# One addition per pair for the halo columns of an up-projection's convolution, with their products made once per block

## The chip, the cores and the metric

The kernel runs on one core of a Trainium2 chip. The metric is the device time of one execution in microseconds, the median of three runs. TensorE (PE) multiplies matrices, VectorE (DVE), ScalarE (ACT) and GpSimd (POOL) work element by element, SyncE (SP) issues the DMAs.

## The reference, cut to what matters

One layer of a bidirectional encoder over 2048 positions with width 1024: a mixer of windowed attention and a state space scan, then a feed-forward part with a convolution over positions. The change touches the feed-forward part:

```python
def dwconv(u, w, b):
    """Centred depthwise conv over positions. u (B,S,C), w (K,C), b (C,)."""
...
  h = rmsnorm(x, norm2_g[l])
  u = dwconv(h @ w_up[l].astype(h.dtype), ffn_conv_w[l], ffn_conv_b[l])
  gate, val = jnp.split(u, 2, axis=-1)
  x = x + (jax.nn.silu(gate) * val) @ w_down[l].astype(h.dtype)
```

The convolution has three taps (FFN_CONV = 3), D_FF is 2816, all in float32. An output position needs its own column of h @ w_up, the one before and the one after.

## The kernel before

Positions lie along the free axis, in four blocks of TB = 512 (j = 0 to 3). For each block the feed-forward part goes through 22 pairs of 128 channels (NPAIR), a gate half and a value half each, in six groups. The four parts of a pair's way are:

- **Weights.** `next_w` (L145) keeps two weight tiles ahead. `w_split` (L130) makes two tiles of each raw tile: ACT casts the high part (`whi`, L141), then POOL, for a few early tiles DVE, subtracts it from the raw one for the low part (`wlo`, L142). Each tag has two buffers, so a new `whi` starts when PE has finished with the one two before.
- **Product.** `up_mm` (L1046) makes two banks of 512 columns for a pair, each from 8 x 3 matmuls: high by high (L106), high weight by low input (L107), low weight by high input (L108).
- **Convolution.** `up_unit` (L1056) has the three taps and the bias. The sum is kept one position behind, so column t of the tile `fa` is position t - 1 of the block: an activation on ACT takes the middle tap and the bias (L1067), and two scalar_tensor_tensor of 128x510 and 128x511 on DVE the others (`tap`, L1065). The first two columns of `fa` also need the last two columns of the block before, kept in `hal` for each pair and half (copied by L1079). For j > 0 two more taps, of 128x2 and 128x1, add them in (L1071 and L1072, both recorded as L1065). The last block makes one more column (L1074).
- **Gate.** ACT makes the tanh of the gate half (L1087), DVE two products (L1088, L1089), and `tail` splits the result into a high part `f` (ACT, L1092) and a low one (DVE, L1093). `flush` puts a pair's tail behind the next pair's taps.

Between these, `pace` steps the attention and the scan of the next block, whose instructions share all engines. Down-projections (`dn_b`, `dn`), the output projection of the next block (`wo_b`, with its split input `m_hi`, `m_lo`, L989 and L990) and its norm follow each other at the end of a block. The tile framework orders each engine's queue with a timeline of its own, from the program's order and the estimated times; on the chip each engine takes its queue in order, and semaphores stand between engines.

Of the kernel before, what the change touches and what calls it, by code (L numbers as in the profile page):

```python
# [10 lines left out]
F32 = mybir.dt.float32  # L11
F32R = mybir.dt.float32r
AF = mybir.ActivationFunctionType
ALU = mybir.AluOpType
# [3 lines left out]
P = 128  # L18
# [9 lines left out]
NPAIR = DFF // P  # L28
# [29 lines left out]
def block_kernel(ctx: ExitStack, tc: tile.TileContext, a: dict, out: bass.AP):  # L58
    nc = tc.nc

    cpool = ctx.enter_context(tc.tile_pool(name="cpool", bufs=1))
# [9 lines left out]
    def const(name, shape):  # L71
        t = cpool.tile(shape, F32, tag=name, name=name)
        nc.sync.dma_start(t, a[name])
        return t
# [11 lines left out]
    ptot = cpool.tile([P, 6, H], F32, tag="ptot", name="ptot")  # L86
    sv, pv, lv = (cpool.tile([P, 8, 2], F32, tag=n, name=n) for n in ("sv", "pv", "lv"))
    hal = cpool.tile([P, NPAIR, 2, 2], F32, tag="hal", name="hal")

    def dram(name, shape):  # L90
        return dpool.tile(shape, F32, tag=name, name=name)
# [19 lines left out]
    V, G, A, T = nc.vector, nc.gpsimd, nc.scalar, nc.tensor  # L111
# [176 lines left out]
    def flush():  # L288
        for f in pend:
            f()  # L290
        pend.clear()
# [6 lines left out]
    fcw = const("fcw", [P, NPAIR, 2, 4])  # L298
# [757 lines left out]
    def up_unit(j, pr, fs, idx, ps):  # L1056
        last = j == NB - 1
        acc = tpool.tile([P, 2 * FW], F32, tag="t1024", name=f"fa{j}_{pr}", bufs=5)
        acc = acc.rearrange("p (i n) -> p i n", i=2)
        for i in range(2):  # L1060
            w = lambda q: fcw[:, pr, i, q : q + 1]
            ai, u = acc[:, i], ps[i]

            def tap(o, q, src):
                V.scalar_tensor_tensor(o, src, w(q), o, ALU.mult, ALU.add)  # L1065

            A.activation(ai[:, 0:TB], u, AF.Identity, bias=w(3), scale=w(2))  # L1067
            tap(ai[:, 2:TB], 0, u[:, 0 : TB - 2])
            tap(ai[:, 1:TB], 1, u[:, 0 : TB - 1])
            if j > 0:  # L1070
                tap(ai[:, 0:2], 0, hal[:, pr, i, 0:2])  # L1071
                tap(ai[:, 0:1], 1, hal[:, pr, i, 1:2])  # L1072
            if last:
                V.tensor_scalar(  # L1074
                    ai[:, TB : TB + 1], u[:, TB - 1 : TB], w(1), w(3), ALU.mult, ALU.add
                )
                tap(ai[:, TB : TB + 1], 0, u[:, TB - 2 : TB - 1])
            else:
                V.tensor_copy(hal[:, pr, i], u[:, TB - 2 : TB])  # L1079
        n = TB  # L1080
        if last:
            n = FW
            V.memset(acc[:, :, TB + 1 : FW], 0.0)
        flush()

        th = t512(f"fth{j}_{pr}")
        A.activation(th[:, :n], acc[:, 0, :n], AF.Tanh)  # L1087
        V.scalar_tensor_tensor(th[:, :n], th[:, :n], 1.0, acc[:, 0, :n], ALU.add, ALU.mult)  # L1088
        V.tensor_tensor(th[:, :n], th[:, :n], acc[:, 1, :n], ALU.mult)  # L1089

        def tail():
            A.copy(fs[:, idx, 0, :n], th[:, :n])  # L1092
            V.tensor_tensor(fs[:, idx, 1, :n], th[:, :n], fs[:, idx, 0, :n].bitcast(F32), ALU.subtract)  # L1093

        pend.append(tail)

    def down_unit(j, g, cp, fs, w):
        k0, nk = GROUPS[g]
# [258 lines left out]
    def start_side(j):  # L1357
        side.clear()
        due[:] = [0.0, 0.0]
        if j == NB:  # L1360
            return None
        m = new_mixed(j)
        side.extend([(chunks(attn, j, m), RATE[0]), (chunks(ssd, j, m), RATE[1])])
        return m
# [19 lines left out]
    for j in range(NB):  # L1384
        more = j + 1 < NB
        if j > 0:
            mx = start_side(j + 1)
        fss = []
        for g, (k0, nk) in enumerate(GROUPS):
            fs = big.tile([P, SLOT], F32R, tag="big", name=f"f{j}_{g}").rearrange(  # L1390
# [2 lines left out]
            i = 0  # L1393
            if j == 0 and g == 0 and UP2:
# [9 lines left out]
                i = 2  # L1404
# [118 lines left out]
```

## Time and profile before

| what | value |
|---|---|
| runs before | 2463.56, 2461.11, 2459.13 us; median 2461.11 |
| profiled execution, its own time | 2459.2 us |
| its span in the trace | 2457.1 us |
| DVE taps on `hal` | 264, 101 us |
| mean granted clock of TensorE | 0.987 |

The time of the profiled execution is 2.1 us above its span. A row of the trace names the line, the engine, the operation, the tiles written and read with buffer numbers left out, and the shape; a wait is put down to the instruction whose semaphore came last. In a timeline a number in brackets is the idle time of that engine just before the instruction, with what ended it.

### The profile page before, as it was taken

The numbers are of one execution on the slowest core, as the hardware profiler recorded it, in microseconds if no ns is written. First come the engines' busy times: TensorE is split into PE (matmuls) and PEld (weight loads), VectorE is DVE, ScalarE is ACT, GpSimd is POOL, SyncE is SP. The second block draws the span as 40 slices with busy tenths as digits, with TensorE's granted clock in tenths as the row PEclk, the third lists the DMA queues.
The fourth block names the chain that finished last, engine by engine and source line by source line (L and its number), as shares of the span: only waits on it lengthen the run. The fifth ranks groups of instructions, "written<-read, shape, count | busy, mean of one in ns | idle before, by whom it ended". The sixth has DMA issues, their size and how long they took to land.

```text
span 2457.1 us, 31337 instructions
## 1 busy us (share of the span) xinstructions
PE 2347.2 (96%) x11440; PEld 1955.7 (80%) x11440; DVE 1687.5 (69%) x3056; ACT 1075.5 (44%) x1818; POOL 1086.0 (44%) x585
## 2 busy tenths in 40 slices
PE   8999999897999999999999999999999999999997
PEld 6878797776788878778787877787888877788887
DVE  5757777777886684569877675698776556844445
ACT  5444656345454443435443443354444333433334
POOL 1114314463644544455444454555444436544444
PEclk9999999998999999999999999999999999999999
DMA  6567445883444333334434333343342232333332
GB/s 229 166 194 221 134 148 181 253 274 115 130 129 126 117 125 101 124 93 152 123 117 128 122 112 116 92 153 118 114 129 90 86 121 85 121 103 95 95 92 80
DMA packets 172461, 325.82 MB, mean 133 GB/s; under 512 B 12690, under 2 KB 83730, under 8 KB 172308
## 3 DMA queue, kind: packets, MB, share of 16 engines
q1 hardware_dynamic: 172308, 323.83, 41.8%
q8 instruction: 90, 1.47, 0.2%
q14 instruction: 63, 0.52, 0.1%
HBM read 277.77 MB, written 44.71 MB: 131 GB/s over the span
## 4 chain that ended last, share of the span: by engine, by line
PE 45%; DVE 14%; POOL 2%; ACT 2%; issue 2%; DMA 1%; DVEq 0%; POOLq 0%; ACTq 0%
PE up_b L108 8%; PE up_b L107 8%; PE up_b L106 8%; DVE fa L1065 4%; PE dn_b L106 3%; PE dn_b L107 3%; PE dn_b L108 3%; PE dn L107 2%; PE dn L106 2%; PE dn L108 2%; PE wo_b L108 2%; PE wo_b L106 2%; PE wo_b L107 2%; POOL wlo L142 1%; DVE ab L893 1%
## 5 line engine op out<-in xcount | busy, mean ns | idle before, releaser
L142 POOL TENSOR_TENSOR wlo<-wraw,whi 128x1024 fp32r<-128x1024 f32 (+1 forms) x306 | 738.2, 2413 | 895.4 <-ACT whi L141 837.6
L108 PE MATMUL up_b<-h_hi,wlo 128*128 128x512 f32 x1392 | 551.7, 396 | 14.7 <-POOL wlo L142 14.7
L106 PE MATMUL up_b<-h_hi,whi 128*128 128x512 f32 x1392 | 551.3, 397 | 3.4 <-ACT whi L141 2.3
L107 PE MATMUL up_b<-h_lo,whi 128*128 128x512 f32 x1392 | 549.2, 395 | 1.9 <-DVE h_lo L208 1.9
L141 ACT CAST whi<-wraw 128x1024 fp32r<-128x1024 f32 (+1 forms) x330 | 338.9, 1027 | 467.6 <-PE up_b L107 120.9
L1065 DVE SCALAR_TENSOR_TENSOR fa<-up_b,fcw,fa 128x511 f32<-128x511 f32 (+2 forms) x396 | 271.7, 687 | 211.2 <-ACT fa L1067 206.7
L108 PEld LDWEIGHTS up_b<-h_hi,wlo 128*128 128x128 f32 x1392 | 262.4, 189 | 77.7 <-POOL wlo L142 21.1
L106 PEld LDWEIGHTS up_b<-h_hi,whi 128*128 128x128 f32 x1392 | 261.9, 188 | 62.7 <-ACT whi L141 4.9
L107 PEld LDWEIGHTS up_b<-h_lo,whi 128*128 128x128 f32 x1392 | 262.1, 188 | 60.0 <-DVE h_lo L208 3.4
L106 PE MATMUL dn_b<-f,whi 128*128 128x512 f32 x528 | 211.4, 400 | 0.4 <-DVE x L1108 0.2
L107 PE MATMUL dn_b<-f,whi 128*128 128x512 f32 x528 | 208.7, 395 | 0.0
L108 PE MATMUL dn_b<-f,wlo 128*128 128x512 f32 x528 | 204.2, 397 | 0.0
L1092 ACT CAST f<-fth 128x512 fp32r<-128x512 f32 (+1 forms) x88 | 54.6, 620 | 216.5 <-DVE fth L1089 175.5
L1087 ACT ACTIVATE fth<-fa 128x512 f32<-128x512 f32 (+1 forms) x88 | 55.6, 632 | 212.6 <-DVE fa L1065 167.6
L1108 DVE TENSOR_TENSOR x<-x,dn_b 128x512 f32<-128x512 f32 x144 | 97.6, 681 | 59.9 <-PE dn_b L108 59.6
L1067 ACT ACTIVATE fa<-up_b,fcw 128x512 f32<-128x512 f32 x176 | 135.9, 773 | 0.2
L106 PEld LDWEIGHTS dn_b<-f,whi 128*128 128x128 f32 x528 | 99.8, 189 | 22.9 <-DVE x L1108 1.1
L108 PEld LDWEIGHTS dn_b<-f,wlo 128*128 128x128 f32 x528 | 99.3, 188 | 22.5 <-POOL wlo L142 0.2
L107 PEld LDWEIGHTS dn_b<-f,whi 128*128 128x128 f32 x528 | 99.2, 188 | 21.0
L893 DVE SCALAR_TENSOR_TENSOR ab<-ab,ldt,mask 128x128 f32<-128x128 f32 x256 | 95.3, 442 | 21.8 <-DMA ab<-acs_d 21.8
L1065 DVE SCALAR_TENSOR_TENSOR fa<-hal,fcw,fa 128x2 f32<-128x2 f32 (+1 forms) x264 | 101.0, 383 | 4.6
L1093 DVE TENSOR_TENSOR f<-fth,f 128x512 fp32r<-128x512 f32 (+1 forms) x88 | 78.9, 897 | 30.9 <-ACT f L1092 30.1
(333 smaller groups left out, 4880.4 us busy)
## 6 DMA issues: line engine op xcount, KB each, us to landing
wraw<-in_w_up SPq DMA_DIRECT2D x176, 512.0 KB
wraw<-in_w_dn SPq DMA_DIRECT2D x64, 512.0 KB
wraw<-in_w_out SPq DMA_DIRECT2D x36, 512.0 KB
ab<-acs_d SPq DMA_DIRECT2D x32, 512.0 KB
wraw<-in_w_ch SPq DMA_DIRECT2D x28, 512.0 KB
wraw<-in_w_dn SPq DMA_DIRECT2D x32, 384.0 KB
ak<-ks_d SPq DMA_DIRECT2D x14, 768.0 KB
xt<-in_x SPq DMA_DIRECT2D x16, 512.0 KB
```

The source lines that it names most:

```text
L106: nc.tensor.matmul(ps, whi, xhi, start=first, stop=False)
L107: nc.tensor.matmul(ps, whi, xlo, start=False, stop=False)
L108: nc.tensor.matmul(ps, wlo, xhi, start=False, stop=last)
L141: A.copy(hi[:, :m], raw[:, :m])
L142: (V if i < WV or i in WVS else G).tensor_tensor(lo[:, :m], raw[:, :m], hi[:, :m].bitcast(F32), ALU.subtract)
L893: (G if i < SUBP[0 if first else 1] else V).scalar_tensor_tensor(ab[:, i, d], ab[:, i, d], ldt[:, d, c, h : h + 1], mask3[:, 2 * d * P : ( ...
L1065: V.scalar_tensor_tensor(o, src, w(q), o, ALU.mult, ALU.add)
L1067: A.activation(ai[:, 0:TB], u, AF.Identity, bias=w(3), scale=w(2))
L1087: A.activation(th[:, :n], acc[:, 0, :n], AF.Tanh)
L1092: A.copy(fs[:, idx, 0, :n], th[:, :n])
L1093: V.tensor_tensor(fs[:, idx, 1, :n], th[:, :n], fs[:, idx, 0, :n].bitcast(F32), ALU.subtract)
L1108: V.tensor_tensor(xv, xv, ps[i], ALU.add)
```

## The change

A second tile `cor` holds, for each pair and half, what the block before adds to the first two columns: `hal` column 0 by tap weight 0 plus `hal` column 1 by tap weight 1 for column 0, and `hal` column 1 by tap weight 0 for column 1. `halo_cor` makes it for all 22 pairs and both halves with three instructions on DVE ahead of each block j > 0, the second of which writes over the first column of `hal`. In `up_unit` one addition of 128x2x2 for both halves takes the place of the four taps, behind the loop over the halves.

```diff
+    cor = cpool.tile([P, NPAIR, 2, 2], F32, tag="cor", name="cor")
...
             tap(ai[:, 1:TB], 1, u[:, 0 : TB - 1])
-            if j > 0:
-                tap(ai[:, 0:2], 0, hal[:, pr, i, 0:2])
-                tap(ai[:, 0:1], 1, hal[:, pr, i, 1:2])
             if last:
...
             else:
                 V.tensor_copy(hal[:, pr, i], u[:, TB - 2 : TB])
+        if j > 0:
+            V.tensor_tensor(acc[:, :, 0:2], acc[:, :, 0:2], cor[:, pr], ALU.add)
         n = TB
...
+    def halo_cor():
+        m = NPAIR * 2
+        hv, cv = (t.rearrange("p a i q -> p (a i) q") for t in (hal, cor))
+        wv = fcw.rearrange("p a i q -> p (a i) q")
+        V.tensor_tensor(cv, hv, wv[:, :, 0:1].broadcast_to([P, m, 2]), ALU.mult)
+        V.tensor_tensor(hv[:, :, 0:1], hv[:, :, 1:2], wv[:, :, 1:2], ALU.mult)
+        V.tensor_tensor(cv[:, :, 0:1], cv[:, :, 0:1], hv[:, :, 0:1], ALU.add)
...
             mx = start_side(j + 1)
+            halo_cor()
```

The engines' orders move with it. DVE, pair 5 of block 1 (`fa_5` is its convolution, `fth_5` its tanh and products, `up_5_b` its two banks), before:

```order
L1065 SCALAR_TENSOR_TENSOR fa_5_9930<-hal,fcw,fa_5_9930 128x2
L1065 SCALAR_TENSOR_TENSOR fa_5_9930<-hal,fcw,fa_5_9930 128x1
L1079 COPY hal<-up_5_b_9880 128x2
L1088 SCALAR_TENSOR_TENSOR fth_5_9945<-fth_5_9945,fa_5_9930 128x512
L1065 SCALAR_TENSOR_TENSOR fa_5_9930<-up_5_b_9881,fcw,fa_5_9930 128x510
L798 TENSOR_TENSOR mixed_9190<-po_1_9724,ao_1_9951 64x2x128 x2
L1065 SCALAR_TENSOR_TENSOR fa_5_9930<-up_5_b_9881,fcw,fa_5_9930 128x511
L1065 SCALAR_TENSOR_TENSOR fa_5_9930<-hal,fcw,fa_5_9930 128x2
L808 TENSOR_REDUCE ass_9957<-asq_9955 128x128
L1065 SCALAR_TENSOR_TENSOR fa_5_9930<-hal,fcw,fa_5_9930 128x1
L1079 COPY hal<-up_5_b_9881 128x2
L1089 TENSOR_TENSOR fth_5_9945<-fth_5_9945,fa_5_9930 128x512
```

The taps on `hal` follow each half's long taps. The same queue now:

```order
L1066 SCALAR_TENSOR_TENSOR fa_5_9919<-up_5_b_9869,fcw,fa_5_9919 128x511
L1077 COPY hal<-up_5_b_9869 128x2
L924 TENSOR_TENSOR ab_1_10054<-ab_1_10054 128x4x128
L1066 SCALAR_TENSOR_TENSOR fa_5_9919<-up_5_b_9870,fcw,fa_5_9919 128x510
L1066 SCALAR_TENSOR_TENSOR fa_5_9919<-up_5_b_9870,fcw,fa_5_9919 128x511
L1077 COPY hal<-up_5_b_9870 128x2
L1079 TENSOR_TENSOR fa_5_9919<-fa_5_9919,cor 128x2x2
L1088 SCALAR_TENSOR_TENSOR fth_5_9931<-fth_5_9931,fa_5_9919 128x512
L940 TENSOR_TENSOR yt_1_9851<-yo_1_9852,ea_9325 128x512
L1089 TENSOR_TENSOR fth_5_9931<-fth_5_9931,fa_5_9919 128x512
```

The first product (L1088), which stood between the halves, now stands behind both. ACT for the same pair, before:

```order
L1067 ACTIVATE fa_5_9930<-up_5_b_9880,fcw 128x512
L1092 CAST f_1_9746<-fth_4_9824 128x512
L877 ACTIVATE ea_10871<-nacs 128x16
L1087 ACTIVATE fth_5_9945<-fa_5_9930 128x512
L141 CAST whi<-wraw 128x1024
L1067 ACTIVATE fa_5_9930<-up_5_b_9881,fcw 128x512
L795 COPY ao_1_9951<-po_1_9724 64x512
L806 ACTIVATE asq_9955<-mixed_9190 128x512
L141 CAST whi<-wraw 128x1024
L1092 CAST f_1_9746<-fth_5_9945 128x512
```

The tanh stands ahead of a `whi` and the second activation. The same queue now:

```order
L1068 ACTIVATE fa_5_9919<-up_5_b_9869,fcw 128x512
L899 ACTIVATE ab_0_10052<-ab_0_10052 128x1024
L899 ACTIVATE ab_1_10054<-ab_1_10054 128x1024
L142 CAST whi<-wraw 128x1024
L1068 ACTIVATE fa_5_9919<-up_5_b_9870,fcw 128x512
L1087 ACTIVATE fth_5_9931<-fa_5_9919 128x512
L878 ACTIVATE ea_10839<-nacs 128x16
L1092 CAST f_1_9738<-fth_5_9931 128x512
L142 CAST whi<-wraw 128x1024
```

The tanh stood between the two activations of its pair; now it stands behind both, and `f` of the same pair stands ahead of the next `whi`. DVE at the end of block 1, with the changed kernel's three new instructions (L1101 to L1103); before, the last two taps on `hal` of pair 21 stood behind the last `m_lo` there:

```order
L991 SCALAR_TENSOR_TENSOR m_lo<-mixed_9191,gv,m_hi 128x512 x2
L1116 TENSOR_TENSOR x_1_8691<-x_1_8691,dn_4_1_b_12572 128x512
L991 SCALAR_TENSOR_TENSOR m_lo<-mixed_9191,gv,m_hi 128x512
L1079 TENSOR_TENSOR fa_21_12510<-fa_21_12510,cor 128x2x2
L1116 TENSOR_TENSOR x_1_8691<-x_1_8691,dn_4_1_b_12573 128x512
L1101 TENSOR_TENSOR cor<-hal,fcw 128x88
L1088 SCALAR_TENSOR_TENSOR fth_21_12522<-fth_21_12522,fa_21_12510 128x512
L1102 TENSOR_TENSOR hal<-hal,fcw 128x44
L1089 TENSOR_TENSOR fth_21_12522<-fth_21_12522,fa_21_12510 128x512
L1103 TENSOR_TENSOR cor<-cor,hal 128x44
L1093 TENSOR_TENSOR f_5_12283<-fth_21_12522,f_5_12283 128x512
L1030 TENSOR_TENSOR x_2_12602<-x_2_12602,wo_0_b_12618 128x512
```

They stand between the instructions of the block's last pair, ahead of the first addition of the output projection.

## Rows read from the trace of the kernel before

**Rows 1.** Page, part 1: busy time, share, instructions of each engine.

```profile
PE 2347.2 (96%) x11440; PEld 1955.7 (80%) x11440; DVE 1687.5 (69%) x3056; ACT 1075.5 (44%) x1818; POOL 1086.0 (44%) x585
```

**Rows 2.** Up-projections of blocks 1-3: PE, PEld, DVE, ACT, POOL busy; clock; DMA share, GB/s.

```profile
1100.00:1490.00 390.00, 380.48 (x1755) 310.98 (x1753) 300.59 (x580) 174.74 (x308) 186.72 (x98) 1.00 0.39 124
1593.00:1983.00 390.00, 384.48 (x1779) 314.53 (x1778) 287.86 (x570) 177.96 (x312) 185.03 (x95) 1.00 0.37 115
2066.00:2406.00 340.00, 337.57 (x1831) 291.37 (x1832) 187.46 (x421) 122.80 (x157) 157.10 (x70) 0.99 0.33 100
```

**Rows 3.** Waits of PE in those stretches: us in total, times, longest.

```profile
PE up_b L108 <- POOL wlo L142: 4.0, 4, 1.7
PE up_b L106 <- ACT whi L141: 1.6, 2, 1.0
...
PE up_b L108 <- POOL wlo L142: 2.2, 3, 1.0
PE up_b L106 <- ACT whi L141: 0.7, 1, 0.7
...
PE up_b L108 <- POOL wlo L142: 4.3, 3, 2.8
```

**Rows 4.** Timeline, block 1, 1167 to 1182: start us, us, what, [idle before].

```profile
1167.70 3.60 DVE L1065 SCALAR_TENSOR_TENSOR fa<-hal,fcw,fa 128x2 f32<-128x2 f32 x2
...
1168.90 2.39 POOL L142 TENSOR_TENSOR wlo<-wraw,whi 128x1024 fp32r<-128x1024 f32 x1
...
1177.01 0.63 ACT L1087 ACTIVATE fth<-fa 128x512 f32<-128x512 f32 x1 [4.05 <-DVE fa L1065]
...
1177.54 1.03 ACT L141 CAST whi<-wraw 128x1024 fp32r<-128x1024 f32 x1
...
1178.62 0.50 PE L106 MATMUL up_b<-h_hi,whi 128*128 128x512 f32 x1 [0.64 <-ACT whi L141]
...
1181.08 0.50 PE L108 MATMUL up_b<-h_hi,wlo 128*128 128x512 f32 x1 [1.03 <-POOL wlo L142]
```

**Rows 5.** DVE's groups by form: busy us, mean ns of one | idle before.

```profile
L1065 DVE SCALAR_TENSOR_TENSOR fa<-hal,fcw,fa 128x1 f32<-128x1 f32 x132 | 54.3, 412 | 2.5
...
L1089 DVE TENSOR_TENSOR fth<-fth,fa 128x512 f32<-128x512 f32 x66 | 52.8, 800 | 0.0
...
L1065 DVE SCALAR_TENSOR_TENSOR fa<-hal,fcw,fa 128x2 f32<-128x2 f32 x132 | 46.8, 354 | 2.1
...
L1079 DVE COPY hal<-up_b 128x2 f32<-128x2 f32 x132 | 20.5, 155 | 2.7
```

**Rows 6.** Instructions on the tile hal: durations in ns, min/median/max.

```profile
L1065 DVE SCALAR_TENSOR_TENSOR fa<-hal,fcw,fa x264: 201/219/2339, 1100.1 to 2410.2; 128x2 f32<-128x2 f32 x131, 128x1 f32<-128x1 f32 x1
```

**Rows 7.** Two small additions on DVE, lines 769 and 760: ns min/median/max.

```profile
L769 DVE TENSOR_TENSOR rsm<-rsm,es x32: 149/161/2371, 285.6 to 1898.6; 128x4 f32<-128x4 f32 x32
...
L760 DVE TENSOR_TENSOR es<-vecs,mxs x32: 148/1425/2364, 282.9 to 1895.0; 128x4 f32<-128x4 f32 x32
```

**Rows 8.** Timeline, block 1, 1182 to 1185.

```profile
1182.53 2.41 POOL L142 TENSOR_TENSOR wlo<-wraw,whi 128x1024 fp32r<-128x1024 f32 x1 [1.51 <-ACT whi L141]
1182.76 2.20 DVE L1065 SCALAR_TENSOR_TENSOR fa<-hal,fcw,fa 128x1 f32<-128x1 f32 x1
```

**Rows 9.** Waits of PE from 1080 on: the one ahead of the output projection.

```profile
PE wo_b L106 <- DVE x L1108: 10.4, 2, 5.2
```

**Rows 10.** Timeline of a quiet pair at the end of block 1.

```profile
1489.78 0.83 ACT L141 CAST whi<-wraw 128x768 fp32r<-128x768 f32 x1 [0.29 <-PE up_b L107]
...
1491.33 1.53 DVE L1065 SCALAR_TENSOR_TENSOR fa<-up_b,fcw,fa 128x510 f32<-128x510 f32 x2 [1.11 <-ACT fa L1067]
...
1493.46 0.63 ACT L1087 ACTIVATE fth<-fa 128x512 f32<-128x512 f32 x1 [2.17 <-DVE fa L1065]
...
1495.33 0.83 ACT L141 CAST whi<-wraw 128x768 fp32r<-128x768 f32 x1 [1.23 <-PE up_b L107]
```

**Rows 11.** Page, part 5: the cast f on ACT.

```profile
L1092 ACT CAST f<-fth 128x512 fp32r<-128x512 f32 (+1 forms) x88 | 54.6, 620 | 216.5 <-DVE fth L1089 175.5
```

## The prediction

> **What bounds the kernel now.** I read the page's busy shares first. TensorE (PE) is busy 2347.2 of 2457.1 us, VectorE (DVE) 69% [rows 1]. So the question is not how much DVE work the change removes, but how much of PE's idle time is caused by it. The change acts only in the blocks j = 1, 2, 3, after about 1075 us; ahead of that the kernel is the same. The table of busy time by stretch, cut to the three up-projection stretches, comes next [rows 2]: PE is idle for 390 - 380.48 = 9.5 us, 390 - 384.48 = 5.5 us and 340 - 337.57 = 2.4 us, 17.4 us in all, at a granted clock of 1.00, 1.00 and 0.99 (2.4 GHz). DVE is busy 77%, 74% and 55% there. That 17.4 us is nearly all there is to win in these stretches.
>
> Then the list of PE's waits in the same stretches [rows 3]. Its largest entries are the split weights: PE waits for wlo from POOL 4.0, 2.2 and 4.3 us, and for whi from ACT 1.6 and 0.7 us, 12.8 us. In the third stretch 2.8 us of the 4.3 are one wait at the very start of the block, before any tap of that block runs. So 10.0 us in 12 waits are left, 0.8 us each. The remaining idle time of the first two stretches is attention and scan steps (9.5 - 4.0 - 1.6 = 3.9 us and 5.5 - 2.2 - 0.7 = 2.6 us).
>
> How do weights come late because of taps? The timeline shows it [rows 4]. Two taps on hal, together some 0.45 us when nothing is in the way, take 3.60 us from 1167.70 and end at 1171.30, as POOL's wlo does (1168.90 + 2.39 = 1171.29). DVE falls behind, the tanh of the next pair waits on ACT 4.05 us for a tap, the whi cast queued behind that tanh starts at 1177.54, and PE stands 0.64 us for whi and then 1.03 us for the wlo made from it. This is the path from a tap to PE: tap, tanh in ACT's queue, whi, wlo, PE.
>
> **The change part by part.** *Removed:* 264 taps on hal, four in each of the 22 pairs of three blocks: 132 of 128x2 at 354 ns and 132 of 128x1 at 412 ns [rows 5], 46.8 + 54.3 = 101.1 us of DVE. The median tap is 219 ns, the longest 2339 ns [rows 6], so 264 x 0.219 = 58 us is the work itself and 43 us is standing still as in [rows 4].
>
> *Added, 66 additions of 128x2x2.* The trace has no such instruction. The nearest are two additions of 128x4 in SBUF [rows 7], with medians of 161 and 1425 ns: 66 of them are 11 us at the one and 94 us at the other. I take the mean tap, 101.1 / 264 = 0.383 us, because the addition stands where the taps stood and, like them, reads two SBUF tiles and writes one while POOL works: 25 us.
>
> *Added, three instructions ahead of each block, nine in all* (128x88 and two of 128x44). Bounds: 0.16 us each by the faster of the two additions [rows 7] (1.4 us), 2.3 us each by the longest tap (21 us); I take 0.4 us, 4 us in all. In the order they stand behind the last m_lo of the block before, among that block's last instructions, where DVE next waits for the output projection; that wait covers them. Without that cover they would cost those 4 us, three times 1.2 us.
>
> DVE's sum: -101 + 25 + 4 = -72 us, between -89 and +14. The Trainium skill, Perfetto Trace Analysis, section Optimizing Scalar/DVE Operations, gives about 60 ns of overhead for a DVE instruction on SBUF; by that figure 189 fewer instructions would be an estimated 11 us, and the sum would be a sixth of mine; here the rows show 219 ns and more for one.
>
> *What of it reaches PE.* -72 us over 66 pairs is 1.1 us less DVE work for each pair, and each of the 12 weight waits is 0.8 us. If every one were due to a DVE queue late by that much, all 10.0 us would go. Two things speak against taking it whole. First, a blocked tap is partly a blocked DVE, not a tap: the tap at 1182.76 takes 2.20 us because wlo runs on POOL from 1182.53 for 2.41 us [rows 8]; without the tap, the product L1089 that follows in the queue also reads two SBUF tiles and may meet the same wlo. Second, the tanh, which had to wait for the four taps of the gate half, now has to wait for one addition behind both halves. On the tanh's path two taps (0.44 us unhindered) go, and the second half's two long taps (1.53 us in a quiet pair [rows 10]) and a copy (0.16 us [rows 5]) and the addition come. I take half of the 10.0 us as won: -5 us.
>
> *What is given back.* The scheduler has put the tanh behind the second activation, and often f, the cast of the same pair's product, right behind the tanh. Counted in ACT's order over the three blocks, the places where tanh and f of one pair both stand between two successive whi casts go from 4 to 12. At such a place whi waits for tanh, two DVE products and f. I charge the 8 new ones 0.25 us each, a third of a present wait: +2 us. PE's order moves too, since the attention and scan matmuls are placed by the same scheduler; I cost that at 0 +- 3 us.
>
> *What stays.* The two largest PE waits of the transitions, 5.2 us each for x L1108 ahead of the output projection, do not hang on taps: they are two waits, 10.4 us [rows 9], and in the order the last pair's second taps on hal stand behind the m_lo that this x stands behind too. The last block's tail is the same.
>
> **The sum:** -5 + 2 = -3 us. The profiled execution took 2459.2 us, 1.9 us under the median of the three runs, 2461.1; so 2456 for one such as that and 2458 for the median, which I give.
>
> **The rivals.**
>
> *More than that.* With 1.1 us less DVE work per pair the scan and attention steps come earlier too. For it: the chain through DVE [rows 4], and DVE 77% and 74% busy in just the two stretches that hold 15 of the 17.4 us idle. Against it: the tap that meets wlo whoever stands in the queue [rows 8]. All 10.0 us of weight waits less the 2 us given back, and 1 to 2 us of the other 6.5: -9 us, 2452.
>
> *The block moves on.* What the taps stood for, the two products and the addition stand for next, and the 58 us of real work lie beside PE. Nothing reaches PE: 2461, +- 2.
>
> *Slower: the tanh is late.* In a quiet pair the tanh starts at 1493.46 and the next whi at 1495.33, after 1.23 us of waiting for PE [rows 10]; successive whi casts follow PE at 1489.78 and 1495.33, 5.55 us apart. whi (1.03) and wlo (2.39, both [rows 4]) must fit in that, so there are 2.1 us more to lose before PE stands: 3.4 us in all. The new path takes 1.53 + 0.16 - 0.44 = 1.25 us out of it ahead of the addition, and at the twelve places with f another 2.2 us (two products of up to 0.80 us [rows 5] and f's 0.62 us [rows 11]). Where POOL then blocks the addition for 2 us, PE stands. Twelve such stalls of 0.8 us, less the 2 us gained elsewhere, are +8 us: 2469. It decides from the point where tanh's and f's delay exceeds 3.4 us. The page named above says in the same section that work which causes bubbles on an engine that is not the busy one may be done sooner if instructions are broken up, and that grouping pays where the engine is saturated; by that rule, with DVE at 55 to 77%, merging is the wrong way and this rival would hold. The trace bears it out as far as ACT stands waiting for taps [rows 4]; it speaks against it in that four taps at the mean of 0.383 us hold DVE 1.5 us a pair, on both sides of the tanh.
>
> That the change does not do what it says I leave out: the new order has 264 taps fewer and 75 instructions more.
>
> **How the numbers follow.** Forecast 0.40, more 0.22, moves on 0.20, slower 0.18. About 0.2% of the time, 5 us, is what a measurement can tell from no change. Faster by more than that: nearly all of the second case and three in ten of the first, 0.33. Slower by more: most of the fourth and a little of the rest, 0.19. Within it: 0.48. The range reaches to -12 us (all weight waits and a third of the others) and to +9 us (the slower rival and 1 us): 2449 to 2470; about 0.13 lies outside. The bounds of DVE's sum lie within: -89 us is the second case with a little more relief, +14 us is 0.2 us more DVE work a pair, the slower rival's case.
>
> **What would show it.** DVE's busy time near 1687.5 - 72 = 1615 us, with 189 instructions fewer on the page. The addition's mean between 161 and 1425 ns, near 380. PE idle in the three stretches down from 17.4 to about 14 us. In PE's waits the wlo and whi entries at about 9 us in place of 12.8, the transition waits still 5.2 us. Tanh waiting on ACT for the addition. Wrong would be: weight waits above 18 us in sum (the slower rival), or under 5 us (the larger gain), or a changed transition, which no term here holds.

## The result and the profile after

The changed kernel takes 2446.93 us in the median of four runs (2445.09 to 2450.18), beside 2462.34 us for the kernel before (2459.13 to 2464.98, four runs). The ratio is 0.9937, 95% interval [0.9919, 0.9955]: 15.4 us or 0.63% faster. That is below the range of 2449 to 2470 us, five times the forecast gain of 3 us, and beyond the 9 us of the rival "More than that". The direction was right; the size was not, and not by one term alone.

The profiled execution of the change took 2447.2 us, its span 2445.0 us. Its busy times, against [rows 1]:

```profile
PE 2344.5 (96%) x11440; PEld 1955.9 (80%) x11440; DVE 1666.2 (68%) x2867; ACT 1075.4 (44%) x1818; POOL 1091.7 (45%) x585
```

The 189 instructions are gone, but DVE is busy only 21 us less, not 72. To see where the 15 us come from I cut both traces at the first and last matmul on `up_b` of each block. The three up-projections lie between these, a transition is what stands between the last of one block and the first of the next (the rest of the down-projection, the output projection, the norm). In the table each stage has its length in us and, in brackets, the sum of PE's listed waits in it. Block 1 starts at 1089.4 us in the trace before and at 1093.2 us after. The code up to there is the same but for three small instructions, and that start lies between 1089 and 1096 us in the profiles of this study, so only what follows is compared.

| kernel | up 1 | transition 1-2 | up 2 | transition 2-3 | up 3 | tail | sum |
|---|---|---|---|---|---|---|---|
| before | 405.7 (11.7) | 87.4 (5.2) | 395.2 (7.6) | 85.7 (5.2) | 342.2 (4.3) | 51.4 | 1367.7 |
| the change | 401.6 (9.1) | 83.1 (2.0) | 394.3 (7.1) | 81.2 (1.2) | 339.6 (3.0) | 52.0 | 1351.8 |
| difference | -4.1 | -4.3 | -0.9 | -4.5 | -2.6 | +0.6 | -15.9 |

A second profile of the same changed kernel (an experiment below) has 400.2, 82.9, 394.3, 81.4, 341.0 and 51.9: one stage is good to about 1.4 us. These two profiles differ by one stretch of 3.4 us at the lower of TensorE's two clock levels (1.2 GHz), which lies in block 1 in the one and in block 3 in the other. So **-8.8 us come from the two transitions and -7.6 us from the three up-projections.**

**The up-projections.** PE's waits in the three stages, which answer to [rows 3] (us in total, times, longest):

```profile
PE up_b L109 <- POOL wlo L143: 4.6, 4, 1.9
PE pt L782 <- DVE pl L786: 2.4, 1, 2.4
PE sc L754 <- DVE mxs L756: 1.1, 1, 1.1
...
PE up_b L109 <- POOL wlo L143: 3.7, 3, 1.6
PE pt L782 <- DVE pl L786: 2.3, 1, 2.3
PE sc L754 <- DVE mxs L756: 1.1, 1, 1.1
...
PE up_b L109 <- POOL wlo L143: 3.0, 2, 2.8
```

The waits for split weights are 4.6 + 3.7 + 3.0 = 11.3 us, and none is for `whi` any more. The same view over the whole stages before:

```profile
PE up_b L108 <- POOL wlo L142: 6.2, 6, 1.7
...
PE up_b L106 <- ACT whi L141: 1.6, 2, 1.0
...
PE up_b L108 <- POOL wlo L142: 4.3, 5, 1.3
...
PE up_b L106 <- ACT whi L141: 0.7, 1, 0.7
...
PE up_b L108 <- POOL wlo L142: 4.3, 3, 2.8
```

That is 17.1 us, so these waits fell by 5.8 us. The windows of [rows 3] were a little shorter and showed 12.8. Of the 2.8 us at the start of block 3 nothing went, as the prediction had it. In exchange PE waits twice for the low part of an attention tile (`pl`), 4.7 us. All waits together fell from 23.6 to 19.2 us. The other 3 us of the 7.6 stand in no listed wait, nor in the clock: in both kernels it is at the lower level for 6.8 us of these stages.

**The transitions.** The end of block 1, the timeline before (start us, us, what, idle time just ahead and its releaser):

```profile
1502.77 5.36 POOL L142 TENSOR_TENSOR wlo<-wraw,whi 128x1024 fp32r<-128x1024 f32 x2 [4.67 <-ACT whi L141]
...
1503.73 4.94 DVE L990 SCALAR_TENSOR_TENSOR m_lo<-mixed,gv,m_hi 128x512 fp32r<-128x512 f32 x2
...
1508.60 0.68 DVE L1108 TENSOR_TENSOR x<-x,dn_b 128x512 f32<-128x512 f32 x1
...
1509.42 0.76 PE L106 MATMUL wo_b<-m_hi,whi 128*128 128x512 f32 x1 [5.21 <-DVE x L1108]
...
1509.86 0.21 DVE L1065 SCALAR_TENSOR_TENSOR fa<-hal,fcw,fa 128x2 f32<-128x2 f32 x1
...
1510.83 0.16 DVE L1079 COPY hal<-up_b 128x2 f32<-128x2 f32 x1
```

and the same place in the trace after:

```profile
1502.48 5.44 POOL L143 TENSOR_TENSOR wlo<-wraw,whi 128x1024 fp32r<-128x1024 f32 x2 [4.67 <-ACT whi L142]
...
1503.44 0.14 DVE L1077 COPY hal<-up_b 128x2 f32<-128x2 f32 x1
1503.51 4.96 DVE L991 SCALAR_TENSOR_TENSOR m_lo<-mixed,gv,m_hi 128x512 fp32r<-128x512 f32 x2
...
1504.45 0.50 PE L107 MATMUL wo_b<-m_hi,whi 128*128 128x512 f32 x1 [0.49 <-ACT whi L142]
...
1508.39 0.67 DVE L1116 TENSOR_TENSOR x<-x,dn_b 128x512 f32<-128x512 f32 x1
```

Two `m_lo`, 0.74 us each when nothing is in the way, take DVE 4.9 us in both, while two `wlo` run on POOL (5.36 and 5.44 us). What differs is the copy of pair 21's last two columns. It is the last reader of that pair's PSUM bank. Before, it writes over the `hal` columns that the pair's taps read, so it had to follow those taps, and they stood behind `m_lo`: it ran at 1510.83. Now nothing binds it to the addition, it stands right behind the long taps, at 1503.44, and the bank is free. In the two built programs the second bank of the output projection's first piece is accordingly a different one: before, it is the bank of a down-projection, which the `x` at 1508.60 has to read first, and now it is that of pair 21. PE no longer waits for `x`. Its listed waits in the two transitions fell from 10.4 to 3.2 us, 7.2 of the 8.8 us.

The clock adds to it. The rows of busy time by stretch of 20 us (us, then PE, PEld, DVE, ACT and POOL busy, PE's granted clock, DMA), before:

```profile
1500.00:1520.00 20.00, 14.79 (x56) 11.63 (x55) 12.93 (x17) 6.04 (x8) 7.40 (x4) 0.83 0.50 175
```

and after:

```profile
1500.00:1520.00 20.00, 19.50 (x83) 14.91 (x82) 14.03 (x21) 6.33 (x10) 8.04 (x4) 1.00 0.56 194
```

Before, the clock is at the lower of its two levels (1.2 GHz) from 1506.9 us on, in the middle of the wait, for 6.8 us; matmuls on `wo_b` then take 0.63 us in place of 0.39. Some 4.3 us of that lie behind the wait, about 2 us of work lost. After, PE has no long wait there and the clock stays at 1.00 (2.4 GHz).

**What DVE does now.** The taps' own cost before is in [rows 5, 6]. What took their place, by the instructions on the tile `cor` after (durations in ns, min/median/max):

```profile
L1079 DVE TENSOR_TENSOR fa<-fa,cor x66: 147/160/1379, 1112.4 to 2397.3; 128x4 f32<-128x4 f32 x66
L1101 DVE TENSOR_TENSOR cor<-hal,fcw x3: 233/240/241, 1026.4 to 1987.7; 128x88 f32<-128x88 f32 x3
L1103 DVE TENSOR_TENSOR cor<-cor,hal x3: 192/195/197, 1027.9 to 1989.2; 128x44 f32<-128x44 f32 x3
```

The additions have a median of 160 ns, the nine instructions of `halo_cor` 0.19 to 0.24 us. What grew in exchange are four groups of other instructions. Groups by form (busy us, mean ns), before:

```profile
L1093 DVE TENSOR_TENSOR f<-fth,f 128x512 fp32r<-128x512 f32 x66 | 55.8, 845 | 22.7 <-ACT f L1092 22.0
...
L776 DVE TENSOR_SCALAR sm<-sm,rsm 128x384 f32<-128x384 f32 x88 | 53.6, 669 | 0.6
...
L1093 DVE TENSOR_TENSOR f<-fth,f 128x514 fp32r<-128x514 f32 x22 | 23.2, 1053 | 8.2 <-ACT f L1092 8.2
```

and after:

```profile
L777 DVE TENSOR_SCALAR sm<-sm,rsm 128x384 f32<-128x384 f32 x88 | 74.0, 893 | 0.5
L1093 DVE TENSOR_TENSOR f<-fth,f 128x512 fp32r<-128x512 f32 x66 | 67.5, 1022 | 14.0 <-ACT f L1092 13.1
L1089 DVE TENSOR_TENSOR fth<-fth,fa 128x512 f32<-128x512 f32 x66 | 63.1, 956 | 0.8
...
L1093 DVE TENSOR_TENSOR f<-fth,f 128x514 fp32r<-128x514 f32 x22 | 38.2, 1738 | 0.4 <-ACT f L1092 0.4
```

These four grew by 20.4, 11.7, 10.3 (from 52.8, [rows 5]) and 15.0 us, 57 us in all, in the same number of instructions on the same shapes. They now meet `wlo` more often: of the 88 `f`, 40 take over 1.4 times as long as the shortest, and in 35 of these a `wlo` of POOL ends; before, it was 16 and 11. It is the place of the one addition that goes with this, not the absence of the taps. Two kernels described below, e3 and e4, have no taps either, but nothing in them makes the tanh wait for both halves, and there the four groups come to 183.5 and 179.2 us; before they were 185.4, with the change 242.8. In e3:

```profile
L777 DVE TENSOR_SCALAR sm<-sm,rsm 128x384 f32<-128x384 f32 x88 | 57.0, 701 | 0.7
...
L1093 DVE TENSOR_TENSOR f<-fth,f 128x514 fp32r<-128x514 f32 x22 | 19.9, 906 | 9.9 <-ACT f L1092 9.8
```

### The profile page after: what moved, and what is told of

It is laid out like the page before. It is cut to its first block, busy times and chain, and to the rows that moved or that the text cites. A ratio compares the mean times of both kernels' runs of the same rounds, so it can differ in the third digit from the quotient of the medians.

```text
span 2445.0 us, 31146 instructions
## 1 busy us (share of the span) xinstructions
PE 2344.5 (96%) x11440; PEld 1955.9 (80%) x11440; DVE 1666.2 (68%) x2867; ACT 1075.4 (44%) x1818; POOL 1091.7 (45%) x585
## 4 chain that ended last, share of the span: by engine, by line
PE 52%; DVE 7%; POOL 3%; DMA 1%; issue 1%; ACT 1%; DVEq 0%; POOLq 0%; ACTq 0%
PE up_b L109 10%; PE up_b L107 10%; PE up_b L108 10%; PE dn_b L107 3%; PE dn_b L109 3%; PE dn_b L108 3%; POOL wlo L143 2%; PE dn L109 2%; PE dn L108 2%; PE dn L107 2%; DVE m_lo L991 1%; PE wo_b L109 1%; DVE sm L777 1%; PE wo_b L108 1%; PE wo_b L107 1%
## 5 line engine op out<-in xcount | busy, mean ns | idle before, releaser
L109 PE MATMUL up_b<-h_hi,wlo 128*128 128x512 f32 x1392 | 550.4, 396 | 11.4 <-POOL wlo L143 11.4
L1066 DVE SCALAR_TENSOR_TENSOR fa<-up_b,fcw,fa 128x510 f32<-128x510 f32 (+2 forms) x396 | 271.2, 686 | 246.5 <-ACT fa L1068 242.3
L109 PEld LDWEIGHTS up_b<-h_hi,wlo 128*128 128x128 f32 x1392 | 262.3, 188 | 73.4 <-POOL wlo L143 15.4
L1068 ACT ACTIVATE fa<-up_b,fcw 128x512 f32<-128x512 f32 x176 | 135.9, 774 | 11.4 <-DVE fth L1089 11.1
L1087 ACT ACTIVATE fth<-fa 128x512 f32<-128x512 f32 (+1 forms) x88 | 55.6, 632 | 164.7 <-DVE fa L1079 115.6
L894 DVE SCALAR_TENSOR_TENSOR ab<-ab,ldt,mask 128x128 f32<-128x128 f32 x256 | 104.3, 475 | 19.0 <-DMA ab<-acs_d 19.0
L109 PEld LDWEIGHTS dn_b<-f,wlo 128*128 128x128 f32 x528 | 99.4, 188 | 21.9
L108 PEld LDWEIGHTS dn_b<-f,whi 128*128 128x128 f32 x528 | 99.2, 188 | 21.1
L1093 DVE TENSOR_TENSOR f<-fth,f 128x512 fp32r<-128x512 f32 (+1 forms) x88 | 105.7, 1201 | 14.4 <-ACT f L1092 13.5
L107 PE MATMUL pj_b<-h_hi,whi 128*128 128x512 f32 x208 | 84.9, 409 | 15.1 <-ACT h_hi L236 6.8
```

Source lines behind the costliest of these rows:

```text
L107: nc.tensor.matmul(ps, whi, xhi, start=first, stop=False)
L108: nc.tensor.matmul(ps, whi, xlo, start=False, stop=False)
L109: nc.tensor.matmul(ps, wlo, xhi, start=False, stop=last)
L894: (G if i < SUBP[0 if first else 1] else V).scalar_tensor_tensor(ab[:, i, d], ab[:, i, d], ldt[:, d, c, h : h + 1], mask3[:, 2 * d * P : ( ...
```

## The experiments

My theory had two causes: the copy of the last pair, freed from the taps, lets the output projection start (transitions), and fewer small instructions between the long taps and the products let the weights come earlier (up-projections). Rivals: it is the load alone, with the transitions a by-product; it is the order of all copies; or it is the place of the tanh. The stages of the table below are those of the table above. The last three columns are sums over up 1 to up 3 in us: PE's listed waits, those for split weights among them, and the time at the lower clock. Before, they were 23.6, 17.1 and 6.8; with the change 19.2, 11.3 and 6.8. Ahead of block 1 the engines' orders are the same but for the few instructions of `halo_cor`, in all but g2, whose copies stand on ACT in block 0 too.

| experiment | median us | ratio to before, 95% | up 1 | 1-2 | up 2 | 2-3 | up 3 | waits | weights | low clock |
|---|---|---|---|---|---|---|---|---|---|---|
| e1, taps kept, all copies free | 2462.27 | 0.9997 [0.9981, 1.0013] | 405.0 | 85.2 | 400.8 | 81.1 | 340.8 | 26.1 | 14.8 | 6.8 |
| f1, taps kept, last copy free | 2455.17 | 0.9976 [0.9967, 0.9986] | 405.5 | 83.6 | 394.7 | 81.2 | 341.6 | 20.2 | 15.2 | 10.2 |
| e2, change, all copies bound | 2465.04 | 1.0018 [1.0006, 1.0031] | 404.8 | 88.4 | 396.9 | 87.0 | 341.0 | 23.0 | 12.4 | 10.2 |
| f2, change, last copy bound | 2457.84 | 0.9989 [0.9979, 0.9998] | 400.9 | 88.7 | 394.5 | 86.4 | 341.2 | 19.1 | 10.8 | 6.8 |
| f4, change again | 2447.00 | 0.9944 [0.9933, 0.9956] | 400.2 | 82.9 | 394.3 | 81.4 | 341.0 | 19.1 | 11.4 | 6.8 |
| e3, change, addition per half | 2450.50 | 0.9950 [0.9931, 0.9969] | 400.6 | 83.6 | 392.9 | 81.5 | 343.2 | 18.6 | 11.3 | 6.8 |
| e4, change, no addition | 2442.96 | 0.9921 [0.9896, 0.9946] | 397.3 | 83.0 | 391.2 | 82.7 | 344.3 | 13.6 | 9.4 | 13.7 |
| f3, change, 132 more | 2468.63 | 1.0033 [1.0022, 1.0045] | 413.0 | 82.9 | 404.3 | 81.3 | 342.2 | 30.5 | 17.3 | 30.7 |
| g1, change, four additions | 2455.23 | 0.9974 [0.9962, 0.9986] | 404.2 | 83.6 | 397.1 | 81.5 | 343.2 | 21.9 | 12.3 | 13.7 |
| g2, change, copies on ACT | 2452.54 | 0.9968 [0.9957, 0.9980] | 404.5 | 83.6 | 393.8 | 81.3 | 341.0 | 21.1 | 14.2 | 6.8 |

Take from a kernel's three up-projections its listed waits and half of its time at the lower clock, as an estimate of what that costs (matmuls on `wo_b` took 0.63 us there in place of 0.39), and 1112 to 1117 us are left in all twelve profiles, while the three stages themselves spread over 27 us. So most of what separates these kernels there is PE's waits and the lower clock. The waits for weights are 14.8 to 17.1 us in the three kernels that keep the taps, 17.3 in f3, which puts instructions of the taps' shapes back, and 9.4 to 12.4 in the seven others whose copies stay on DVE.

### e1: the kernel before, with all copies free of the taps

Two `hal` tiles take turns, so that the copy need not follow the taps; the taps stay.

```diff
-                V.tensor_copy(hal[:, pr, i], u[:, TB - 2 : TB])
+                V.tensor_copy(hals[j % 2][:, pr, i], u[:, TB - 2 : TB])
+            if j > 0:
+                tap(ai[:, 0:2], 0, hals[1 - j % 2][:, pr, i, 0:2])
+                tap(ai[:, 0:1], 1, hals[1 - j % 2][:, pr, i, 1:2])
```

> The kernel before with two tiles for the halo columns in turn, so that the copy of a pair's last two columns no longer has to follow the four taps that read the old ones; all 264 taps stay. Theory A (the PSUM bank of the last pair is released earlier, because the copy that reads it last stands ahead of the last m_lo): PE's two waits of 5.2 us ahead of the output projection go, about -8.7 us against before, 2453 to 2455 us, and the waits in the three up-projection stretches stay near 11.7, 7.6 and 4.3 us. Theory B (the gain comes from less work on DVE): no change, 2462 us.

The time is that of the kernel before. The transitions alone fell by 2.2 and 4.6 us, but the up-projection of block 2 grew by 5.6, and with it an attention wait, longest 3.8 us where it was 0.5 in that stage (the list of PE's waits from 1080 us on):

```profile
PE up_b L108 <- POOL wlo L142: 14.7, 15, 2.8
PE pt L781 <- DVE pl L785: 5.5, 2, 3.8
...
PE dn_b L106 <- DVE hal L1076: 1.8, 1, 1.8
```

Block 2 also has 6.8 us at the lower clock there, where the kernel before had none in that stage. The 5.2 us wait for `x` is not among the waits. So free copies take that wait away, but in 21 of 22 pairs they also move other work, to a loss here. The total alone would have thrown the theory out; the stages kept it.

### f1: the kernel before, with the last pair's copy free

The same for pair 21 alone.

```diff
+            end = pr == NPAIR - 1
+            if end and not last:
+                V.tensor_copy(hls[j % 2][:, i], u[:, TB - 2 : TB])
             if j > 0:
-                tap(ai[:, 0:2], 0, hal[:, pr, i, 0:2])
-                tap(ai[:, 0:1], 1, hal[:, pr, i, 1:2])
+                old = hls[1 - j % 2][:, i] if end else hal[:, pr, i]
+                tap(ai[:, 0:2], 0, old[:, 0:2])
+                tap(ai[:, 0:1], 1, old[:, 1:2])
```

> The kernel before with two small tiles in turn for the last pair's halo columns alone, so that only pair 21's copy may stand ahead of its taps; all 264 taps and the copies of the other 21 pairs stay as they were. Theory A (the two transitions gain from the earlier release of that pair's PSUM bank, whatever DVE has to do): both waits of 5.2 us go, the way from the end of the up-projection to the next one is 83 and 81 us in place of 87.4 and 85.7, -8 to -9 us against before, 2453 to 2454 us; the up-projections stay at 1143 us in sum. Rival (the release only moves the wait to the next block, as it looked for all pairs): 2460 to 2463 us.

Faster by 0.24%, some 6 us (3 to 8 by the interval), a little less than expected. Both transitions are those of the change (83.6 and 81.2 us), the up-projections those of the kernel before. PE's waits from 1493 to 1590 us:

```profile
PE wo_b L109 <- POOL wlo L143: 1.7, 1, 1.7
PE wo_b L107 <- ACT whi L142: 0.9, 2, 0.5
PE up_b L109 <- POOL wlo L143: 0.8, 1, 0.8
```

### e2 and f2: the change, with the copies bound again

In e2 the sums are kept in `hal` itself, so that every copy must follow the addition; in f2 only pair 21's.

```diff
-            else:
-                V.tensor_copy(hal[:, pr, i], u[:, TB - 2 : TB])
         if j > 0:
-            V.tensor_tensor(acc[:, :, 0:2], acc[:, :, 0:2], cor[:, pr], ALU.add)
+            V.tensor_tensor(acc[:, :, 0:2], acc[:, :, 0:2], hal[:, pr], ALU.add)
+        if not last:
+            for i in range(2):
+                V.tensor_copy(hal[:, pr, i], ps[i][:, TB - 2 : TB])
```

f2 does this where the following holds:

```diff
+        bound = pr == NPAIR - 1 and j > 0 and not last
```

> The changed kernel with the sums kept in the tile of the halo columns itself, so that the copies have to follow the addition, as they had to follow the taps before; the addition of 128x2x2 per pair stays. Theory A (release): PE's waits ahead of the output projection come back, 5 us or more each, +8 to +11 us against the change, 2455 to 2458 us. Theory B (less DVE work): as the change, 2447 us.

> The changed kernel with only the last pair's copies of blocks 1 and 2 bound behind its addition. Theory A: the waits of 4.6 to 5.2 us ahead of the output projections are back, +8 to +10 us against the change, 2455 to 2457 us, while the up-projections keep their 1135 to 1137 us. Rival (the transitions are not the larger part): 2447 to 2451 us.

f2 gives back 10.8 us of the change's gain, with the transitions at 88.7 and 86.4 us and the up-projections of blocks 1 and 2 within 1 us of the change's. The wait is back (PE's waits from 1493 to 1590 us):

```profile
PE wo_b L107 <- DVE x L1121: 4.6, 1, 4.6
```

and so is the lower clock (busy time by stretch, the 20 us at that place):

```profile
1499.00:1519.00 20.00, 15.22 (x52) 11.62 (x53) 14.05 (x22) 6.51 (x9) 6.34 (x4) 0.83 0.48 170
```

With f1 this is shown from both sides: **the last pair's copies, instructions of 0.16 us, decide over the transitions**, whether the taps are there or not. The banks go with it: in the built program of f1 the second bank of the output projection's first piece is that of pair 21, as in the change, and in f2 it is that of a down-projection, as before. e2 has the late transitions too, but lies 7 us above the range that was expected. It also loses in the up-projections of blocks 1 and 2, 4.6 and 2.6 us against f4's profile: the place of the other copies counts there too, 7 us between e2 and f2. e1 and f1 lie some 5 to 7 us apart with the opposite sign. In the profiles these differences are mostly PE's listed waits: 23.0 us in e2 and 19.1 in f2, 26.1 in e1 and 20.2 in f1.

### f4 and e3: the change again, and one addition per half

f4 is the change, unaltered, run in the same batch as f1 to f3.

> The changed kernel itself, beside the other three on the same chip: 2445 to 2449 us.

It repeats at 2447.0 us. e3 asks whether the tanh's place costs anything: each half has its own addition, and the tanh need not wait for the second half.

```diff
-        if j > 0:
-            V.tensor_tensor(acc[:, :, 0:2], acc[:, :, 0:2], cor[:, pr], ALU.add)
+            if j > 0:
+                V.tensor_tensor(ai[:, 0:2], ai[:, 0:2], cor[:, pr, i], ALU.add)
```

> The changed kernel with one addition of 128x2 for each half, right behind its taps and copy, so that the tanh of the gate half waits for that half alone, as before: 132 additions in place of 66. If the late tanh costs time in the up-projections, as the prediction had it: 2 to 4 us faster than the change, 2443 to 2445. If a tanh behind both halves keeps the weight casts of ACT's queue free, which would be the opposite: 3 to 6 us slower, 2450 to 2453. The 66 more additions are 11 us of DVE work at 0.16 us each, hidden.

It is not told apart from the change: the median lies in the range of the slower case, but the interval of its ratio holds that of f4 whole, and a few us either way cannot be seen at this width. Yet DVE is 30 us less busy:

```profile
PE 2347.1 (96%) x11440; PEld 1956.8 (80%) x11440; DVE 1635.8 (67%) x2933; ACT 1077.4 (44%) x1818; POOL 1080.9 (44%) x585
```

So the late tanh by itself costs PE nothing that shows, though it costs DVE the 57 us on the four groups above, and DVE's busy time is no measure of what PE gets. The Trainium skill, Perfetto Trace Analysis, section Optimizing Scalar/DVE Operations, says that where VectorE is not saturated but causes bubbles on other engines, breaking up instructions may let work be done sooner; cutting the one addition in two gained nothing here.

### e4: the change without the addition

The additions and `halo_cor` are left out, and with them the neighbouring block's contribution to the first two columns.

```diff
-        if j > 0:
-            V.tensor_tensor(acc[:, :, 0:2], acc[:, :, 0:2], cor[:, pr], ALU.add)
...
-            halo_cor()
```

> The changed kernel without the addition and without the three instructions ahead of each block: the neighbouring block's contribution to the first two columns is left out. What the additions still cost: 66 at about 0.2 us are 13 us of DVE work. If they are hidden: as the change, 2445 to 2449 us. If their place ahead of the tanh matters: 2 to 5 us faster.

2443.0 us in the median of four runs: by this, what is left of the contribution costs some 4 us, but the interval overlaps the change's, so the size is not shown. The transitions do not need it. In the profile the up-projections of blocks 1 and 2 gain 3 us each against f4; the third reads 344.3 us with 6.8 us at the lower clock.

### f3 and g1: the number of small instructions

f3 adds three tap-shaped instructions per pair in blocks 1 and 2, behind the copies, 132 in all; they write columns that nobody reads. g1 makes the one addition four, of a quarter each.

```diff
+                if j > 0:
+                    V.scalar_tensor_tensor(
+                        ai[:, TB : TB + 2], cor[:, pr, i], w(0), ai[:, 2:4], ALU.mult, ALU.add
+                    )
+                    if i == 0:
+                        V.scalar_tensor_tensor(
+                            ai[:, TB : TB + 1], cor[:, pr, i, 1:2], w(1), ai[:, 4:5], ALU.mult, ALU.add
+                        )
```

```diff
-            V.tensor_tensor(acc[:, :, 0:2], acc[:, :, 0:2], cor[:, pr], ALU.add)
+            for _ in range(4):
+                V.scalar_tensor_tensor(
+                    acc[:, :, 0:2], cor[:, pr], 0.25, acc[:, :, 0:2], ALU.mult, ALU.add
+                )
```

> The changed kernel with three instructions per pair of blocks 1 and 2 that have the taps' shapes put back at the taps' places, writing to columns that nobody reads: DVE has 132 small instructions more, the copies and the addition stay as in the change. If less DVE work is what shortened the up-projections: blocks 1 and 2 lose what they gained, +4 to +8 us against the change, 2451 to 2455 us, with PE's waits for wlo, whi, scan and attention back near 19 us in these two. If it is the order alone: 2446 to 2449 us. The transitions stay at 83 and 81 us either way.

> The change, with four additions of 128x2x2 at the place of the one, each of a quarter of cor (198 more DVE instructions in blocks 1 to 3, all behind the copies, so that the order at the end of a block stays that of the change). It keeps the change's transitions and gives back the number of DVE instructions. If the number of small DVE instructions between the long taps and the products is what the up-projections lose by: stages of the up-projections of blocks 1 and 2 some 5 to 12 us longer than the change's in sum, transitions near 83 and 81 us without the 5.2 us wait, and a time of 2452 to 2459 us, most of the way back to before. Rival: the number does not matter and the up-projections gained by their changed order alone: the time of the change, 2447 us, within 3 us. Second rival: the last pair's longer chain makes the transitions late again, with the 5.2 us wait back: over 2460 us.

f3 is 21.6 us slower than the change, far above both ranges that were expected. Its up-projections grew by 12.8 and 10.0 us against f4; the transitions and the third block, where nothing was added, stayed. The instructions themselves are like the taps of [rows 6] in their medians (instructions on the tile `cor`, ns):

```profile
L1079 DVE SCALAR_TENSOR_TENSOR fa<-cor,fcw,fa x88: 207/221/2365, 1103.2 to 2007.5; 128x2 f32<-128x2 f32 x88
...
L1083 DVE SCALAR_TENSOR_TENSOR fa<-cor,fcw,fa x44: 203/220/2417, 1103.8 to 1991.6; 128x1 f32<-128x1 f32 x44
```

and PE waits more for `wlo` and `pl` than the 11.4 and 4.7 us of the change (PE's waits from 1080 us on):

```profile
PE up_b L109 <- POOL wlo L143: 15.9, 13, 2.8
PE pt L782 <- DVE pl L786: 8.1, 2, 4.1
...
PE up_b L107 <- ACT whi L142: 1.5, 2, 0.7
```

The waits are not the whole of it. In the three up-projections f3's clock is at the lower level for 30.7 us, the change's for 6.8. One place of it (busy time by stretch; the clock stands behind POOL's busy time):

```profile
1630.00:1645.00 15.00, 11.18 (x44) 9.15 (x45) 13.83 (x19) 6.78 (x10) 8.15 (x5) 0.77 0.20 70
```

Of the 24.0 us that the three stages are longer than with the change, 11.3 are listed waits, and half of the added time at the lower clock, some 12 us by estimate, is nearly all the rest.

g1 is 8 us slower than the change: 198 instructions more, the transitions within a microsecond of the change's, the up-projections +4.0, +2.8 and +2.2 us against f4. ACT's tanh, at the additions of the same line, waited 115.6 us in the change and 160.9 now:

```profile
ACT fth L1090 <- DVE fa L1080: 160.9, 55, 6.5
```

With four additions a pair g1 has as many small instructions per block, 88, as the kernel before had taps, in the order of the change. Its three up-projections add up to 404.2 + 397.1 + 343.2 = 1144.5 us; before they were 1143.1, with the change 1135.5 (1135.5 again in f4). **So four additions in place of one cost as much as the whole gain of the up-projections**, and what g1 keeps, 7 us, is the transitions'. But they do not bring back the waits that the change had taken away (PE's wait for `wlo` from 1080 us on, 11.4 us in the change, and none for `whi`):

```profile
PE up_b L109 <- POOL wlo L143: 12.3, 9, 2.8
```

Of g1's 9.0 us, 2.7 are listed waits of all kinds, some 3.4 by estimate the lower clock (13.7 us in place of 6.8), and the rest is neither. The four additions also follow one another on the same columns ahead of the tanh; whether their number or the length of this chain counts is not told apart. f3 shows that there is no one price per instruction: it also has 88 per block in blocks 1 and 2 (three and the addition in each pair), and its stages there are 7.3 and 9.1 us longer than those of before. Why the change's order takes the load inside the halves so much worse is not shown.

### g2: the copies on ACT

A version to beat the change: 132 instructions less on DVE.

```diff
-                V.tensor_copy(hal[:, pr, i], u[:, TB - 2 : TB])
+                A.copy(hal[:, pr, i], u[:, TB - 2 : TB])
```

> The change, with the copies of the last two columns made by ACT in place of DVE (132 DVE instructions of some 0.16 us fewer in blocks 0 to 2, 132 more on ACT). If the load on DVE sets what the up-projections lose, the time falls by 2 to 6 us under the change's, to 2441 to 2445 us. Rival: ACT's queue, which the casts whi stand in, is the one that counts, and each copy of 0.2 us stands ahead of a cast: PE waits for whi and the wlo behind it more, 2449 to 2453 us. The transitions keep the change's 83 and 81 us in either case, since the copy of the last pair does not stand behind m_lo.

The rival held: 5.6 us slower than the change, inside its range. The copies stand in ACT's queue behind the long taps and ahead of `whi`, and ACT waits there (ACT's waits, 1090 to 2000 us):

```profile
ACT hal L1077 <- DVE fa L1066: 115.0, 66, 4.8
```

PE's wait for `wlo` from 1080 us on is 14.2 us in place of 11.4; in the up-projections it waits for no `whi`. The change stays the fastest kernel of the study that computes everything.

## Why the prediction was wrong

**The step that failed first** is "What stays": "The two largest PE waits of the transitions, 5.2 us each for x L1108 ahead of the output projection, do not hang on taps". They do, by way of a copy. I had looked at what `x` waits for, the `m_lo` ahead of it, and that did not change: two `m_lo` take 4.9 us before and after. I had not asked why the output projection needs that `x`. It needs the bank that `x` reads, and it had that bank because the bank of the last pair was held by a copy behind the taps. The sign was in my own sentence, that the last taps stand behind `m_lo`; the copy behind them and the bank that it holds were missing. The term was 0 and measured -8.8 us. f1 confirms it with all 264 taps in place (-8.3 us in the two transitions), f2 with the taps gone. The prediction did name "a changed transition, which no term here holds" as what would prove it wrong.

**The term that was mis-sized** is what reaches PE in the up-projections: -5 + 2 = -3 us, measured -7.6. The first half was near: the weight waits fell by 5.8 us, and they stay low in the kernels without taps and come back in f3. The +2 us for the later tanh did not appear; e3 finds no cost of the tanh's place that shows. PE's other waits, which the sum left out, rose by 1.4 us. Some 3 us of the 7.6 lie in no wait that the profile lists and not in the clock; that part stays open, so the size of this term is in part luck of the order. g1 does not settle it: it gives the time back without the weight waits. Open, too, is why the places of the other 21 copies bring 4 us of waits more in e2 than in f2, and 6 us more in e1 than in f1, with the copies the other way round.

**DVE's sum**, -72 us, measured -21. Taps gone -101, additions 66 x 0.244 = 16 us (25 forecast), `halo_cor` 2 us (4 forecast): by its parts -83 us, so the instructions that came cost less than forecast. What was left out are some 57 us on four other groups. The prediction had the second half of it in hand, that the tanh now has to wait for one addition behind both halves, and charged that to PE alone. On PE it cost nothing that shows; on DVE it goes with the 57 us: the queue's order moved, and products, `sm` and the low parts of `f` meet `wlo` more often. The rival's argument, that the product behind a tap meets the same `wlo`, does not explain it: e3 and e4, without the taps and without the late tanh, keep the four groups at 183.5 and 179.2 us, and their DVE sums are -52 and -76 us. By the overhead of about 60 ns that the Trainium skill gives for a DVE instruction on SBUF (Perfetto Trace Analysis, section Optimizing Scalar/DVE Operations) 189 fewer make an estimated 11 us; the measured fall of 21 us is nearer to this than to my sum, but by chance: the taps took 101 us, and 57 us came in elsewhere.

**The rivals.** "More than that" had the direction, and its size fits the up-projections alone (-9 forecast, -7.6 measured), but not its terms: the weight waits fell by 5.8 us where it had all 10, and the waits of attention and scan rose from 6.5 to 7.9 us where it had them fall. "The block moves on" did not hold for the time, and on DVE only with the late tanh. "Slower: the tanh is late" found no cost in PE's time; e3, without the late tanh, is no faster. **The range** failed because it was built from cases that all share the transition term of 0: every one of its ends would have been 8.8 us lower with it, and the result lies inside that range.

## What to carry to other kernels

When a small instruction is removed, ask not only what it costs but which instruction had to follow it, and what that one releases. A tiny copy that is the last reader of a PSUM bank can decide where the next stage's matmuls are put, and a wait that names one instruction (`x`) can be there because of another one's place. Compare by stages, with a profile per experiment: e1 had the same total as before, with 6.8 us won in its transitions and 5.6 us lost in block 2. And note PE's waits and the lower clock beside each stage's length: here they made up most of what differed.

## What the runs showed that I had not expected

- Where DVE stands still is set by the order of its queue. With 264 taps gone and one addition behind both halves, the low part `f` of the last block went from 1053 to 1738 ns in the mean, same shape and count; with the taps gone and an addition behind each half (e3) it is 906 ns, at a time that is not told apart.
- 132 instructions of 0.22 us in the median, 72 us of DVE's time as they ran, cost 21.6 us of the whole; 198 of 0.16 us, 52 us as they ran, cost 8 us, on an engine that is idle some 30% of the span. In the first case about half of the cost is the lower clock.
- A PE wait of 5 us was followed by the lower clock for up to 6.8 us, and it began inside the wait (clock 0.83 over 1500 to 1520 us before and 0.83 in f2, 1.00 after).
